# Mixer B's attention: far scores copied by ScalarE into p's row and masked there in one step, o summed in place, four row buffers

## Chip, cores and metric

The kernel runs on one core of a Trainium2 chip. The metric is device time in microseconds of one execution; the time before is the median of three runs.

## Reference

One decoder block over 1024 tokens of width 1024, float32. A combined projection feeds two attention mixers, their normed outputs go through one output projection, and a squared-ReLU MLP of width 4096 follows. The change touches the attention, above all mixer B: eight heads of 64, each query attending in three branches, at distances 0 to 128; at multiples of 4 up to 512; and at multiples of 16 up to 2048, mixed by their softmax denominators.

```python
B_BRANCHES = ((128, 1), (512, 4), (2048, 16))
...
for window, d in B_BRANCHES:
    sub = s // d
    ...
    o, lse = banded_attention(to_sub(q)[:, :, :, None, :], to_sub(k), to_sub(v),
                              window // d, return_lse=True)
...
w = jax.nn.softmax(jnp.stack(lses, axis=0), axis=0)
return jnp.sum(w[..., None] * jnp.stack(outs, axis=0), axis=0)
```

Mixing by denominators is one softmax over all keys in which a key counts as often as branches reach it (1, 2 or 3 times). The kernel does that with one additive mask: "neg" is 1e30 where no branch reaches, 0, −ln 2 or −ln 3 where one, two or three do. Scores are kept negated, so the row's maximum is a minimum, and the exponential uses scale −1.

## The kernel before

**Layout.** Tokens are stored in blocks of 128 with the even tokens of a block first and the odd ones behind. Far keys (two blocks back and more) are reached at even distances only, so of a far block a query in the even half needs the even 64 keys and one in the odd half the odd 64. The score matmul computes whole blocks into a PSUM bank (s_ps, up to 512 columns); from a far block only half is used. Near keys (this block and the one before, 256 columns) are used whole. A row of p for block qb therefore has 64 columns for each far block and 256 near ones, at most 640 in all.

**Work items.** Mixer A has 16 items (group, block); mixer B has 32 items (u, tp, h): a head pair u, a pair tp of query blocks (qb = 2 tp and 2 tp + 1), and a head h in the pair. For each of the two blocks qi of a mixer B item, `s_b` issues: the score matmuls (L1311) in one or two runs of up to four key blocks each, every run in its own bank of two; masking on VectorE (L1345); the exponential on ScalarE with the row's sum (L1353); the reciprocal on VectorE (L1356); and the scaling of p on GpSimd (L1358). `score_parts` splits the masking of a run: for far blocks one instruction for the 64 even rows and one for the 64 odd rows, since each half reads other columns of the bank; for the near blocks one instruction for all rows. Each adds the mask from SBUF to the scores in PSUM, writes p, and carries the running minimum on in "mn" (each leaves a short read-out of mn behind it). A query block with two runs so takes up to five such instructions.

Then `t_pv` follows in one or more chunks of up to 512 columns: TensorE transposes p (pt_ps, L1451), ScalarE rounds it to the high half of ph (L1462), VectorE subtracts to get the low half (L1466), and TensorE multiplies ph by the values (o_ps; L1481 near, L1490 far, L1500 for mixer A). The bank o_ps holds high and low parts in its two column halves (mixer B) and in its row halves. For mixer B, ScalarE copies rows 64 to 127 of the first 256 columns to otmp (L1525), VectorE adds the second 256 columns to it in place (L1529) and the first ones into ot (L1530), and a DMA stores ot to o_dram. Mixer A does it with one copy (L1541) and one add (L1546).

**Buffers.** p's rows: three (NP, r_p); score banks: two (r_s); ot: two (r_ot), and one otmp (r_tmp).

**What sets the order.** A planner inside the program (`Sched`) issues every instruction once, when the program is built. It keeps a clock for each engine, takes for each step a written-down cost (`t_dv(n)` for VectorE, `t_ps(n)` for ScalarE reading PSUM, and so on), and gives each engine next the step that could start first by these clocks. Each engine's queue then runs in the order so written. On TensorE the streams of scores, transposes and value products are mixed with "dense" steps (the input projection pj, later the output projection y_ps), which it prefers or puts back by how far attention has come. A step may name two engines and goes to the one that the planner finds done first; GpSimd has a bonus of 1.5 us there. So a changed cost, step or buffer count moves steps on all engines, also those that the change does not name: the subtractions w_hl of the input weights (L601) are such a step.

**The end.** `finish` (L2324) makes the last sums of each token block in two halves of 512 columns, and for each half sends two DMAs (L2333), one for the even and one for the odd tokens.

Of the kernel before, what the change touches and what calls it, by code (L numbers as in the profile page):

```python
# [19 lines left out]
P = 128  # L20
# [38 lines left out]
CW_MA = CW_MB + 1280  # L59
# [58 lines left out]
def _constants(c):  # L118
# [5 lines left out]
    for i in range(2):  # L124
        back = np.repeat(np.arange(6 + i, i, -1), 64)[None, :]
        far = P * back + 2 * (p % 64 - np.tile(np.arange(64), 6)[None, :])
        d = np.concatenate([np.where(back > 1, far, -1), near], 1)
        mult = ((d >= 0) & (d <= 128)).astype(int)
        mult += (d >= 0) & (d <= 512) & (d % 4 == 0)
        mult += (d >= 0) & (d % 16 == 0)  # L130
        c[:, CW_MB + 640 * i:CW_MB + 640 * i + 640] = neg[mult]
# [268 lines left out]
def hybrid_block(ctx: ExitStack, tc: tile.TileContext, x, positions, w_ada, b_ada, g_attn_post, w_in, w_out,  # L400
# [33 lines left out]
    WR, WS, NP, NV, NK, NQ, NT, NO = 6, 2, 3, 3, 2, 2, 2, 2  # L434
    NF = (1, 1)
    TILED = ()
# [5 lines left out]
    r_v, r_k, r_q, r_p, r_ph, r_ot, r_tmp = Res(NV), Res(0), Res(0), Res(NP), Res(NT), Res(NO), Res(1)  # L442
# [630 lines left out]
    def open_attention():  # L1073
# [14 lines left out]
        masks = mkp.tile([P, 1536], F32, name="masks")  # L1088
        e_mask = load(lambda: nc.sync.dma_start(masks[:], consts[:, CW_MB:CW_MB + 1536]), 786432, prio=-20)
        mask_b = [masks[:, 640 * i:640 * i + 640] for i in range(2)]  # L1090
        mask_a = masks[:, 1280:1536]
# [130 lines left out]
    def t_s(qb, run):  # L1222
        if qb // 2 in TILED:
            return (2 * t_mm(P * (qb // 2)) + 0.18) * (run == 0) + 2 * t_mm(2 * P) * (run == n_runs(qb) - 1)
        a, z = s_runs(qb)[run]
        return 2 * t_mm(P * (z - a))

    def n_runs(qb):
        if qb // 2 in TILED:
            return 2 if qb > 5 else 1  # L1230
        return len(s_runs(qb))
# [16 lines left out]
    UB = 2 * (sum(t_s(qb, r) for qb in range(TB) for r in range(n_runs(qb))) +  # L1248
# [21 lines left out]
    def s_b(i, it, rec):  # L1270
# [6 lines left out]
        for qi in range(2):  # L1277
# [4 lines left out]
            seen = [0, 0]  # L1282
            runs = n_runs(qb)
            for m in range(runs):
                end = m == runs - 1

                def f_s(m=m, qi=qi, qb=qb, w=w, b=b, end=end):
# [7 lines left out]
                    q = [qs[u, qb // 4][:, 2 * h + hl, qb % 4 * P:qb % 4 * P + P] for hl in range(2)]  # L1295
                    if tp in TILED:
                        keys = ks[u][:, h].rearrange("p (b c t) -> p b c t", c=2, t=64)
                        if m == 0:
                            for hl in range(2):
# [29 lines left out]
                for n_, (rows, to, from_, nb) in enumerate(parts):  # L1329
# [3 lines left out]
                    for c_ in range(2):  # L1333
                        seen[c_] += whole or c == c_
# [1067 lines left out]
```

## Time and profile before

| | us |
|---|---|
| median of 3 runs (lowest, highest) | 1112.0 (1110.38, 1113.53) |
| the profiled execution, its own time | 1110.98 |
| its span in the profile | 1109.2 |
| mean granted TensorE clock | 0.997 |

Line numbers L... are those of the program before unless the text says otherwise. In rows of the profile, PE is TensorE's matmuls, PEld its weight loads (which overlap them), DVE is VectorE, ACT ScalarE, POOL GpSimd, SP the queue that issues DMAs. A group's row has line, engine, operation, out<-in, shapes and count; then busy time in us and the mean of one in ns; then the idle time of the engine just before them, and what ended it. CUSTOM_DVE_ANT_0 at L1345 is the masking with its running minimum. A row of waits has who waited, for whom, us in all, how often, and the longest. A row of DMAs has what is moved, the count, the size of one and the median time from issue to landing in us. A row of the timeline has the start and the duration in us.

### The profile page before, as it was taken

Reading aid. Unit: us, or ns where it says so; the run is one execution under the profiler, and the core shown is the slowest. Engines: PE = TensorE matmul, PEld = TensorE weight load, DVE = VectorE, ACT = ScalarE, POOL = GpSimd, SP = SyncE. Lnnn points to the kernel's source line nnn. Section 1 sums busy time; section 2 is a strip of 40 time slices with the busy share of each in tenths; the row PEclk is TensorE's granted clock in tenths of the full one; section 3 lists DMA queues with packets and bytes.
Section 4 is the critical chain, followed back from the end, with each engine's and each line's share of the span. In section 5 each row is a group of like instructions: output and inputs, shape, how many; then the busy total and the mean of one; then the engine's idle time right before and its main releaser. Section 6 shows DMA issues by size and latency. Waiting matters only on the chain.

```text
span 1109.2 us, 15399 instructions
## 1 busy us (share of the span) xinstructions
PE 1086.1 (98%) x5185; PEld 894.8 (81%) x5185; DVE 840.3 (76%) x1616; ACT 614.2 (55%) x1080; POOL 246.8 (22%) x324
## 2 busy tenths in 40 slices
PE   8999999999999899999999999999999999999996
PEld 7788888888787777888888888888888888888885
DVE  7978688788888886689797664898644995537997
ACT  8768676464645556677675244743245632347442
POOL 2158777776642121210000000000000000000003
PEclk9999999999999999999999999999999999999998
DMA  9766677565634825657741379322578013593106
GB/s 350 214 197 196 194 213 238 188 205 165 209 115 147 273 84 171 216 221 263 276 164 38 126 254 346 137 77 76 202 269 296 1 57 119 195 330 135 38 20 152
DMA packets 97950, 198.65 MB, mean 179 GB/s; under 512 B 9776, under 2 KB 35504, under 8 KB 97872
## 3 DMA queue, kind: packets, MB, share of 16 engines
q1 hardware_dynamic: 97872, 197.68, 53.1%
q8 instruction: 41, 0.67, 0.3%
q14 instruction: 37, 0.30, 0.1%
HBM read 141.93 MB, written 33.03 MB: 158 GB/s over the span
## 4 chain that ended last, share of the span: by engine, by line
PE 71%; DVE 13%; DMA 6%; issue 4%; ACT 2%; POOL 2%; SPq 1%; POOLq 0%; DVEq 0%; ACTq 0%
PE mlp_ps L2212 17%; PE mlp_ps L2214 17%; PE mlp_ps L2213 17%; PE pj L978 3%; PE pj L981 3%; PE pj L979 3%; DVE p_sb L1345 2%; DMA wa<-in_w_ada 2%; PE s_ps L1311 2%; DMA o_sb<-o_dram 2%; DMA w_st<-in_w_in 1%; PE s_ps L1401 1%; PE y_ps L1766 1%; PE y_ps L1768 1%; PE y_ps L1767 1%
## 5 line engine op out<-in xcount | busy, mean ns | idle before, releaser
L2212 PE MATMUL mlp_ps<-hw 128*128 128x512 f32 x896 | 348.9, 389 | 0.1
L2213 PE MATMUL mlp_ps<-hw 128*128 128x512 f32 x896 | 348.6, 389 | 0.0
L2214 PE MATMUL mlp_ps<-hw 128*128 128x512 f32 x896 | 348.6, 389 | 0.0
L2214 PEld LDWEIGHTS mlp_ps<-hw 128*128 128x128 f32 x896 | 168.2, 188 | 35.2
L2213 PEld LDWEIGHTS mlp_ps<-hw 128*128 128x128 f32 x896 | 168.2, 188 | 35.1
L2212 PEld LDWEIGHTS mlp_ps<-hw 128*128 128x128 f32 x896 | 168.2, 188 | 35.1 <-DVE u L2249 0.6
L1976 DVE TENSOR_TENSOR hw<-w,hw 128x1024 fp32r<-128x1024 f32 x96 | 114.6, 1221 | 97.6 <-ACT hw L1969 95.9
L1969 ACT CAST hw<-w 128x1024 fp32r<-128x1024 f32 x96 | 97.7, 1048 | 127.5 <-PE mlp_ps L2214 86.8
L2322 POOL TENSOR_TENSOR st<-st,nhalf 128x1 f32<-128x1 f32 x8 | 8.0, 1010 | 591.8 <-DVE st L2320 591.8
L978 PE MATMUL pj<-hw,w_hl 128*128 128x512 f32 x240 | 99.3, 414 | 0.0
L981 PE MATMUL pj<-hw,w_hl 128*128 128x512 f32 x240 | 94.6, 394 | 0.0
L979 PE MATMUL pj<-hw,w_hl 128*128 128x512 f32 x240 | 94.3, 393 | 0.0
L1969 ACT CAST hw<-u 128x1024 fp32r<-128x1024 f32 x48 | 48.6, 1052 | 63.2 <-PE mlp_ps L2214 63.2
L1466 DVE TENSOR_TENSOR ph<-pt_ps,ph 128x512 fp32r<-128x512 f32 (+2 forms) x94 | 57.4, 628 | 22.2 <-ACT ph L1462 21.8
L1976 DVE TENSOR_TENSOR hw<-u,hw 128x1024 fp32r<-128x1024 f32 x48 | 56.9, 1219 | 17.8 <-ACT hw L1969 17.8
L1462 ACT CAST ph<-pt_ps 128x512 fp32r<-128x512 f32 (+2 forms) x94 | 49.1, 541 | 29.7 <-PE pt_ps L1451 25.7
L2270 DVE TENSOR_TENSOR yacc<-yacc,mlp_ps 128x512 f32<-128x512 f32 x96 | 62.0, 682 | 3.3 <-PE mlp_ps L2214 3.3
L1353 ACT ACTIVATE p_sb<-p_sb,mn 128x640 f32<-128x640 f32 (+3 forms) x64 | 42.0, 657 | 33.5 <-DVE mn L1345 30.8
L1358 POOL TENSOR_SCALAR p_sb<-p_sb,den 128x640 f32<-128x640 f32 (+3 forms) x64 | 39.8, 626 | 74.2 <-DVE den L1356 57.3
L1128 POOL TENSOR_TENSOR ada_acc<-ada_acc,wa_st 128x512 f32<-128x512 f32 x42 | 55.5, 1321 | 3.5
L981 PEld LDWEIGHTS pj<-hw,w_hl 128*128 128x128 f32 x240 | 45.1, 188 | 10.2
L1766 PE MATMUL y_ps<-hw,oh 128*128 128x512 f32 x128 | 52.1, 407 | 1.1 <-DVE mn L1345 0.7
(212 smaller groups left out, 1938.3 us busy)
## 6 DMA issues: line engine op xcount, KB each, us to landing
hw<-s_dram SPq DMA_DIRECT2D x84, 512.0 KB, 4.2
wa_st<-in_w_ada SPq DMA_DIRECT2D x32, 512.0 KB, 5.4
w<-in_w_up SPq DMA_DIRECT2D x32, 512.0 KB, 5.8
w<-in_w_down SPq DMA_DIRECT2D x32, 512.0 KB, 7.1
s_dram<-hw SPq DMA_DIRECT2D x28, 512.0 KB, 3.3
qt<-hl SPq DMA_DIRECT2D x40, 256.0 KB, 3.0
w_st<-in_w_in SPq DMA_DIRECT2D x36, 256.0 KB, 3.1
x_sb<-in_x SPq DMA_DIRECT2D x16, 512.0 KB, 5.6
```

The source lines that it names most:

```text
L978: T.matmul(ps, w[:, 0, n], h[0], start=(k == 0), stop=False)
L979: T.matmul(ps, w[:, 1, n], h[0], start=False, stop=False)
L981: T.matmul(ps, w[:, 0, n], h[1], start=False, stop=(k == KC - 1))
L1128: G.tensor_tensor(ada.acc[:, :512], ada.acc[:, :512], wa[:, j], ALU.add)
L1466: V.tensor_tensor(b["ph"][:, 1, :w], b["pt"][:, :w], b["ph"][:, 0, :w].bitcast(F32), ALU.subtract)
L1766: T.matmul(ps[:], b["oh"][:, k], wh[:, c0:c0 + 512], start=(k == 4 * m), stop=False)
L1969: A.copy(out[j][0], flat(src[j]))
L1976: V.tensor_tensor(out[j][1], flat(src[j]), out[j][0].bitcast(F32), ALU.subtract)
L2212: T.matmul(ps[m][:], sh, mh, start=starts and k == 0, stop=False, **kw)
L2213: T.matmul(ps[m][:], sh, ml_, start=False, stop=False, **kw)
L2214: T.matmul(ps[m][:], sl, mh, start=False, stop=k == 3, **kw)
L2270: e = op("DVE", t_dv(512), lambda: V.tensor_tensor(y(), y(), ps[m][:], ALU.add), [e, ml.e_y[tb, n]], gives=gives, prio=1)
```

## The change

- **Masking.** The far columns of each run are now copied by ScalarE, one instruction for the even rows and one for the odd rows, from the bank into p's row, unmasked and compact. The near columns are masked by VectorE from the bank for all rows, as before, but start the minimum anew. When all far copies and the near masking of the row are done, one VectorE instruction over all 128 rows adds the mask to the far columns in place and carries the minimum on. For that, both blocks of an item use one mask; the first block of an item has one far block less, and its unused 64 columns are filled with 1e30 by GpSimd. A bank that holds far blocks only is given back by the second copy; the last one by the near masking, which waits for the copies of its run.
- **o.** ScalarE copies rows 0 to 63 of all 512 columns into ot; VectorE adds rows 64 to 127 of the first 256 columns; then the second 256 columns of ot are added to the first, on VectorE or GpSimd as the planner finds. otmp is gone; mixer A uses ot in the same way.
- **Buffers.** Four for p's rows.
- **Masks.** One table of 640 columns less in the constants and in SBUF.
- **Output.** One DMA for each half of a token block.
- A switch that was off (TILED) is removed.

```diff
-CW_MA = CW_MB + 1280
+CW_MA = CW_MB + 640
...
-    WR, WS, NP, NV, NK, NQ, NT, NO = 6, 2, 3, 3, 2, 2, 2, 2
+    WR, WS, NP, NV, NK, NQ, NT, NO = 6, 2, 4, 3, 2, 2, 2, 2
...
-        masks = mkp.tile([P, 1536], F32, name="masks")
+        masks = mkp.tile([P, 896], F32, name="masks")
...
-                        V.tensor_tensor_reduce(p, src, msk, 1.0, mn[:, n0 - 1:n0] if n0 else BIG, ALU.add, ALU.min,
-                                               mn[:, n0:n0 + 1])
-                    last = n_ == len(parts) - 1
-                    last_mn = op("DVE", t_dv(nb) + 0.06, f_max, [e, e_mask] + ([last_mn] if last_mn else []),
-                                 gives=[(r_s, 1)] if last else [], prio=1)
...
+                far = min(z, qb - 1) - a if tp else 0
+                if far > 0:
+                    for c in range(2):
+                        def f_far(c=c, a=a, far=far, m=m, qi=qi, b=b):
+                            rows = slice(64 * c, 64 * c + 64)
+                            A.copy(rec.p[qi][rows, 64 * a:64 * (a + far)].rearrange("p (b t) -> p b t", t=64),
+                                   b["s", m][rows].rearrange("p (b c t) -> p b c t", c=2, t=64)[:, 0:far, c])
+                        e = op("ACT", t_ps(64 * far) + 0.13, f_far, [e], gives=[(r_s, 1)] if c and not end else [], prio=1)
+                    e_far.append(e)
+                if end:
...
+                        V.tensor_tensor_reduce(rec.p[qi][:, o:w], b["s", m][:, c0:c0 + n], mask_b[:, 640 - w + o:640],
+                                               1.0, BIG, ALU.add, ALU.min, b["mn"][:, 0:1])
+                    last_mn = op("DVE", t_dv(w - o) + 0.2, f_near, [e, e_mask], gives=[(r_s, 1)], prio=1)
+            if tp:
+                n = 64 * (qb - 1)
+                if not qi:
+                    e_far.append(op("POOL", 0.2, lambda n=n: G.memset(rec.p[0][:, n:n + 64], BIG), [e], prio=1))
+
+                def f_max(qi=qi, w=w, b=b, n=n):
+                    V.tensor_tensor_reduce(rec.p[qi][:, 0:n], rec.p[qi][:, 0:n], mask_b[:, 384 - n:384],
+                                           1.0, b["mn"][:, 0:1], ALU.add, ALU.min, b["mn"][:, 1:2])
+                last_mn = op("DVE", t_dv(n) + 0.16, f_max, [last_mn] + e_far, prio=1)
...
-                A.copy(ob["tmp"][:, :256], rec.o[64:128, :256])
+                ob["ot"] = opool.tile([64, 512], F32, name="ot", tag="ot")
+                A.copy(ob["ot"][:], rec.o[0:64])
...
-                V.tensor_tensor(ob["tmp"][:, :256], rec.o[0:64, 256:512], ob["tmp"][:, :256], ALU.add)
-                V.tensor_tensor(ob["ot"][:], rec.o[0:64, :256], ob["tmp"][:, :256], ALU.add)
...
+                V.tensor_tensor(ob["ot"][:, :256], rec.o[64:128, :256], ob["ot"][:, :256], ALU.add)
+
+            def f_o3(eng):
+                return lambda: eng.tensor_tensor(ob["ot"][:, :256], ob["ot"][:, :256], ob["ot"][:, 256:], ALU.add)
...
+            e = op(("DVE", "POOL"), (t_dv(256) + 0.08, t_ptt(256)), (f_o3(V), f_o3(G)), [e], prio=0)
...
-                for c in range(2):
-                    nc.sync.dma_start(dst[c], s.x[64 * c:64 * c + 64, 512 * hf:512 * hf + 512])
+                nc.sync.dma_start(dst, s.x[:, 512 * hf:512 * hf + 512])
```

**VectorE, early in mixer B**, in the program before: the first block (qb = 4) of the item u = 2, tp = 2, h = 0, with its two runs. ISA rows with p_sb are maskings, ISA rows with mn alone their read-outs.

```order
L1345 ISA p_sb,mn<-s_ps,masks 64x192
L1345 ISA mn 64x1
L1345 ISA p_sb,mn<-s_ps,masks 64x192
L1345 ISA mn 64x1
L1345 ISA p_sb,mn<-s_ps,masks,mn 64x64
L1345 ISA mn 64x1
L1345 ISA p_sb,mn<-s_ps,masks,mn 64x64
L1345 ISA mn 64x1
L1529 TENSOR_TENSOR otmp<-o_ps,otmp 64x256
L1530 TENSOR_TENSOR ot<-o_ps,otmp 64x256
L1345 ISA p_sb,mn<-s_ps,masks,mn 128x256
L1345 ISA mn 128x1
```

The same block in the changed program (its own line numbers: L1321 is the near masking, L1330 the one over the far columns, L1492 the add to ot, L598 a subtraction of w_hl):

```order
L1321 ISA p_sb,mn<-s_ps,masks 128x256
L1321 ISA mn 128x1
L598 TENSOR_TENSOR w_hl<-w_st,w_hl 128x512
L1492 TENSOR_TENSOR ot<-o_ps,ot 64x256
L1556 SCALAR_TENSOR_TENSOR wo_st<-wo_st,head,wo_hi 128x1024
L1330 ISA p_sb,mn<-p_sb,masks,mn 128x192
L1330 ISA mn 128x1
```

Five maskings became two, the second with both operands in SBUF, and the second add of o is no longer here.

**ScalarE at the same place**, before: the cast of v_hl of the same projection step, then casts of p (ph), a copy of o (otmp) and exponentials.

```order
L946 CAST v_hl<-pv 128x8x64
L1462 CAST ph<-pt_ps 128x512
L1525 COPY otmp<-o_ps 64x256
L596 CAST w_hl<-w_st 128x512
L1353 ACTIVATE p_sb,den<-p_sb,mn 128x512
```

In the changed program (L1311 there is the copy of far scores, L1489 the copy of o, L1336 the exponential):

```order
L943 CAST v_hl<-pv 128x8x64
L1426 CAST ph<-pt_ps 128x512
L593 CAST w_hl<-w_st 128x512
L1311 COPY p_sb<-s_ps 64x192 x2
L1489 COPY ot<-o_ps 64x512
L1552 ACTIVATE wo_hi<-wo_st,head 128x1024
L1311 COPY p_sb<-s_ps 64x256 x2
L1336 ACTIVATE p_sb,den<-p_sb,mn 128x512
```

Pairs of far copies stand between the casts and the exponentials, and the copy of o has 512 columns.

More of the change, by code (lines that the diff above doesn't have):

```diff
@@ L1539, in f_o1 @@
             def f_o1():
[L1540 to L1542 removed]
+                ob["ot"] = opool.tile([64, 512], F32, name="ot", tag="ot")
+                A.copy(ob["ot"][:], rec.o[64:128])
             def f_o2():
[L1545 to L1547 removed]
+                V.tensor_tensor(ob["ot"][:], rec.o[0:64], ob["ot"][:], ALU.add)
+            e0 = op("ACT", t_ps(512), f_o1, [ep], takes=[(r_ot, 1)], prio=0)
+            e = op("DVE", t_dv(512), f_o2, [e0], gives=[(r_ob, 1)], prio=0)
             def f_st():
```

112 lines of the change are left out of this document (27 added, 85 removed).

## The prediction

> **What bounds the kernel now.** I read the page first, then the busy time by stage, then what TensorE waited for, and only then the durations of the pieces that the change touches.
>
> ```profile
> span 1109.2 us, 15399 instructions
> PE 1086.1 (98%) x5185; PEld 894.8 (81%) x5185; DVE 840.3 (76%) x1616; ACT 614.2 (55%) x1080; POOL 246.8 (22%) x324
> 60.00:166.00 106.00, 105.50 (x578) 87.95 (x576) 81.38 (x223) 77.48 (x216) 79.01 (x121) 1.00 0.68 203
> 166.00:430.00 264.00, 257.58 (x1361) 210.79 (x1359) 215.14 (x718) 148.31 (x316) 132.11 (x153) 1.00 0.55 177
> 430.00:512.00 82.00, 80.37 (x385) 65.78 (x383) 60.58 (x99) 59.30 (x99) 10.96 (x14) 1.00 0.57 205
> 512.00:1100.00 588.00, 586.99 (x2588) 485.47 (x2587) 430.81 (x470) 280.08 (x383) 9.23 (x9) 1.00 0.47 163
> 560.00:600.00 40.00, 40.00 (x178) 33.10 (x178) 35.66 (x35) 23.85 (x32) 0.00 (x0) 1.00 0.26 88
> ```
>
> The columns of the window rows are PE, PEld, DVE, ACT and POOL busy, then clock and DMA. TensorE is busy throughout; mixer A's attention fills about 60 to 166, mixer B's 166 to 430, the output projection 430 to 512, the MLP the rest. The change removes no matmul, so it can only win TensorE's idle time before 512 and the tail after the last matmul. In mixer B's stage that idle time is 264.00 − 257.58 = 6.4 us. It understates the waits: 178 matmuls of 512 columns go in 40 us, one per 0.225 us, yet the record of each lasts 0.389 us (below), so a start may be 0.164 us late before idle time shows.
>
> ```profile
> L2212 PE MATMUL mlp_ps<-hw 128*128 128x512 f32 x896 | 348.9, 389 | 0.1
> 166.27 0.41 PE L1311 MATMUL s_ps<-kt,qt 128*128 128x128 f32 x2
> 166.97 0.50 PE L1500 MATMUL o_ps<-ph,v_hl 128*128 128x512 f32 x1 [0.30 <-DVE v_hl L949]
> ...
> 398.41 0.39 PE L1768 MATMUL y_ps<-hw,ol 128*128 128x512 f32 x1
> 398.86 0.50 PE L1311 MATMUL s_ps<-kt,qt 128*128 128x512 f32 x1
> ```
>
> From the first to the last of these places, 26 starts come over 0.14 us late by the timeline; 6.4 + 26 × 0.164 = **10.7 us** is what TensorE loses in mixer B's stage, and the most that the attention edits can win there. The weight loads name the causes:
>
> ```profile
> PEld o_ps L1481 <- DVE ph L1466: 3.9, 6, 1.3
> PEld s_ps L1311 <- issue: 3.3, 9, 0.6
> PEld s_ps L1311 <- DVE mn L1345: 2.5, 6, 0.8
> PEld o_ps L1490 <- DVE ph L1466: 1.4, 3, 1.0
> PEld pt_ps L1451 <- POOL p_sb L1358: 1.3, 5, 0.3
> ```
>
> Two are VectorE's: 2.5 us for a score bank that the masking (mn L1345) has not yet emptied, and 3.9 + 1.4 = 5.3 us for ph, the low half of p, which stands in VectorE's queue behind such masking. Waiting for p itself costs only 1.3.
>
> **The change part by part: VectorE.** Its rows in mixer B:
>
> ```profile
> L1345 DVE CUSTOM_DVE_ANT_0 p_sb<-s_ps,masks,mn 128x256 f32<-128x256 f32 x48 | 22.8, 477 | 1.8 <-PE s_ps L1311 0.7
> L1345 DVE CUSTOM_DVE_ANT_0 p_sb<-s_ps,masks 64x256 f32<-64x256 f32 x48 | 20.2, 420 | 2.5 <-PE s_ps L1311 1.6
> L1345 DVE CUSTOM_DVE_ANT_0 p_sb<-s_ps,masks,mn 64x128 f32<-64x128 f32 x32 | 11.1, 347 | 1.4 <-PE s_ps L1311 0.7
> L1345 DVE CUSTOM_DVE_ANT_0 p_sb<-s_ps,masks 64x128 f32<-64x128 f32 x32 | 9.0, 286 | 1.1 <-PE s_ps L1311 0.6
> L1345 DVE CUSTOM_DVE_ANT_0 p_sb<-s_ps,masks 64x192 f32<-64x192 f32 x16 | 5.6, 353 | 0.5 <-PE s_ps L1311 0.3
> L1345 DVE CUSTOM_DVE_ANT_0 p_sb<-s_ps,masks,mn 64x64 f32<-64x64 f32 x16 | 4.5, 282 | 0.5
> L1345 DVE CUSTOM_DVE_ANT_0 p_sb<-s_ps,masks 128x256 f32<-128x256 f32 x8 | 3.3, 413 | 0.0
> L1345 DVE CUSTOM_DVE_ANT_0 p_sb<-s_ps,masks 128x128 f32<-128x128 f32 x8 | 2.2, 278 | 0.0
> L1530 DVE TENSOR_TENSOR ot<-o_ps,otmp 64x256 f32<-64x256 f32 x32 | 13.3, 417 | 1.1
> ```
>
> - The 144 half-row maskings go: 20.2 + 11.1 + 9.0 + 5.6 + 4.5 = 50.4 us. The 48 near ones lose their carried minimum: 48 × (477 − 413) ns = 3.1 us.
> - 48 whole-row maskings from SBUF come, eight each of 64, 128, ... 384 columns. No row shows one that reads two SBUF operands; the 128-row forms above give 143 ns + 1.055 ns a column (413 and 278) plus 64 ns for the carried minimum: 8 × (6 × 207 + 1.055 × 1344) ns = 21.3 us.
> - Of the 32 second adds of o, 27 stand in GpSimd's program now: −27 × 417 ns = −11.3 us. Five more w_hl subtractions stand in VectorE's instead, 0.69 us each when undisturbed (18.75 below): +3.4 us.
>
> Net −50.4 − 3.1 + 21.3 − 11.3 + 3.4 = −40.1 us: from 215.1 to 175 of 264 us, 81% to 66%.
>
> **ScalarE** gains 128 copies of half rows, and its copy of o grows from 256 to 512 columns:
>
> ```profile
> L1525 ACT COPY otmp<-o_ps 64x256 f32<-64x256 f32 x32 | 11.8, 369 | 17.4 <-PE o_ps L1490 13.4 <-PE o_ps L1481 3.3 <-DVE ot L1530 0.3
> L1541 ACT COPY otmp<-o_ps 64x512 f32<-64x512 f32 x16 | 9.3, 583 | 8.3 <-PE o_ps L1500 8.1
> ```
>
> That is 155 ns + 0.836 ns a column: 48 × 369 + 16 × 315 + 32 × 262 + 32 × 209 ns = 37.8 us, and 32 × 214 ns = 6.8 us. The copies gather every second 64 columns; the maskings of the same views cost no more than contiguous ones (420 against 413 ns), so I add nothing. ScalarE goes from 148.3 to 193 us, 73%: still beside TensorE.
>
> **GpSimd** gains 27 adds of 64 x 256 and 24 fills of 64 columns. Nearest rows: an add of 128 x 512 at 1332 ns, which bounds one from above; I take half, 0.67, and 0.2 for a fill: 23 us, so 132.1 becomes some 150 with the five subtractions gone (5 × 1.3). It is off the path unless it holds others up, and there the trace has something to say:
>
> ```profile
> 18.75 0.69 DVE L601 TENSOR_TENSOR w_hl<-w_st,w_hl 128x512 fp32r<-128x512 f32 x1
> 230.34 1.79 DVE L601 TENSOR_TENSOR w_hl<-w_st,w_hl 128x512 fp32r<-128x512 f32 x1
> 229.93 1.65 POOL L1128 TENSOR_TENSOR ada_acc<-ada_acc,wa_st 128x512 f32<-128x512 f32 x1
> L1128 POOL TENSOR_TENSOR ada_acc<-ada_acc,wa_st 128x512 f32<-128x512 f32 x28 | 37.3, 1332 | 2.3
> ```
>
> The same subtraction of two SBUF tiles takes 0.69 us with GpSimd idle, and 1.79 when a GpSimd add is running: it ends 0.55 us after that add (231.58 to 232.13). The old maskings read one operand from PSUM; the new whole-row ones read p and the mask, both in SBUF. Each may so wait for what GpSimd is doing: GpSimd is busy half the stage (132.11 of 264), its mean piece is 132.11 / 153 = 0.86 us, so 0.5 × 0.43 = 0.21 us on average and 1.33 at worst; 48 × 0.21 = 10 us. VectorE then stands at 185 of 264, 70%, still under today's 81%.
>
> [...]
>
> **What of this lies on the path.** Score-bank waits, 2.5 us: a bank is now emptied by two ScalarE copies (2 × 369 ns where there were 2 × 420), the last one by two copies and one near masking (2 × 262 + 413 where there were 2 × 347 + 477). Bounds: all of it gone, or as much again if the copies queue behind exponentials; I take −2.5, since VectorE no longer holds the first bank at all. Waits for ph, 5.3 us: they pass ScalarE (its cast) and then VectorE (its subtraction); one gets fuller, the other emptier. Bounds: all gone, −5.3; or later, for in the changed program 17 of the 48 whole-row maskings stand at most two rows ahead of such a subtraction, 17 × 0.21 = +3.6 us by the mean hold-up (17 × 1.33 = 22.6 if every one met the longest piece). I take −0.9, nearer to nothing. The fourth row buffer lets scores run further ahead; p is waited for only 1.3 us, and I count nothing. The loads of the masks (768 to 448 KB) delay no row of TensorE: nothing.
>
> **Tail.** The last output piece is ready at 1104.41; its two DMAs start at 1105.07 and, half of 1.19 later, at 1105.66, behind two others in SP's queue:
>
> ```profile
> 1103.67 0.74 DVE L2324 SCALAR_TENSOR_TENSOR x_sb<-yg,st,x_sb 128x512 f32<-128x512 f32 x1
> 1105.07 1.19 SPq L2333 DMA_DIRECT2D out_x<-x_sb  x2
> out_x<-x_sb SPq DMA_DIRECT2D x32, 128.0 KB, 2.3
> gate_d<-gate_st SPq DMA_DIRECT2D x4, 256.0 KB, 2.8
> ```
>
> One DMA of 256 KB can go at about 1104.5, 1.15 us before the last one of today (1105.66), and lands in 2.8 instead of 2.3: −0.6 us (0 to −1.2).
>
> **Sum.** The profiled execution took 1110.98 us, 1.8 more than its span and 1.0 under the median of the three runs (1112.0; they span 1110.38 to 1113.53), so I leave it uncorrected. 1110.98 − 2.5 − 0.9 − 0.6 = **1107.0 us**. A measurement of this kernel can tell about 0.3%, 3.3 us, from no change; the forecast lies just beyond.
>
> **The rivals.**
> - *The waits only change their names.* ScalarE at 73% takes VectorE's place ahead of ph and of the banks. For it: the waits on "issue" (3.3) and on p stay, and what VectorE loses ScalarE gains nearly one for one (40 and 45 us). Against: no engine would be as full as VectorE is today. Only the tail is won: 1110.4.
> - *Slower: the whole-row masking waits for GpSimd.* Its place is the first part of mixer B, where GpSimd runs 0.76 and 1.3 us pieces of the modulation; its price 17 × 0.21 = 3.6 us of late ph, and nothing won but the tail: 1110.98 + 3.6 − 0.6 = 1114.0. It decides from the point where a held masking plus the subtraction behind it outlasts the matmuls scheduled before o_ps, as the present waits of up to 1.3 us show to be close. Against: VectorE gets 40 us shorter. [...]
> - *All of it goes.* Both VectorE waits and those they carry along vanish, 10.7 us, with the tail: 1099.7. Against: 3.3 us of it is put down to issue.
>
> **How the numbers follow.** Forecast 0.45, unchanged 0.30, slower 0.15, all gone 0.10. Around the forecast its own bounds spread several us, so some four fifths of its chance lies beyond 0.3%: faster 0.37 + 0.10 = 0.47; same 0.08 + 0.28 + 0.02 = 0.38, and slower 0.13 + 0.02 = 0.15, since the slower case may stay within 0.3% (0.02) and the unchanged one may end late (0.02). The range, 1101.0 to 1114.5, leaves out the last rival and the far end of the slower one.
>
> **What the profile will show.** The forecast is right if VectorE in mixer B's stage is near 185 us, ScalarE near 193, the wait of s_ps for mn gone, and the last output DMA starts within 0.2 us of its data. Whole-row maskings much over 0.21 us longer than 143 + 64 + 1.055 a column, ending with GpSimd's pieces, show the hold-up; TensorE's waits for ph above 5.3 us make the prediction wrong on the slow side, new waits for the score copies leave it at no change.

## The result: 5% slower, and all of it behind the last matmul

| | before | changed |
|---|---|---|
| median of 4 runs, us | 1111.19 (1109.29 to 1113.53) | 1167.36 (1167.09 to 1167.69) |
| ratio to before, 95% interval | 1 | 1.0505 (1.0483 to 1.0526) |
| profiled execution, us | 1110.98 | 1167.15 |
| its span, us | 1109.2 | 1165.4 |
| mean granted TensorE clock | 0.997 | 0.972 |

The prediction was 1107.0 us, with a range up to 1114.5: wrong by 60 us and in sign. Line numbers from here on are those of the changed program, unless a row is said to be of another.

The page of the changed kernel, its first lines and the DMA share in 40 slices of the span:

```profile
span 1165.4 us, 15326 instructions
PE 1083.3 (93%) x5185; PEld 894.3 (77%) x5185; DVE 819.0 (70%) x1406; ACT 652.7 (56%) x1208; POOL 266.4 (23%) x366
DMA  9665777463638345667315781336931258410111
```

TensorE is busy for as long as before (1083.3 against 1086.1 us); the span grew around it. The DMA row tells where: the last three slices, some 87 us, all stand at a tenth, right where the output is stored. The stages next (window, its length, then PE, PEld, DVE, ACT, POOL busy, granted clock, DMA share, GB/s):

```profile
60.00:166.00 106.00, 105.45 (x580) 87.98 (x579) 81.49 (x231) 80.60 (x223) 78.11 (x119) 1.00 0.68 208
166.00:430.00 264.00, 256.81 (x1370) 212.31 (x1369) 194.27 (x501) 187.33 (x445) 153.53 (x197) 1.00 0.54 176
430.00:512.00 82.00, 81.62 (x386) 66.79 (x385) 62.77 (x102) 58.75 (x93) 10.05 (x15) 1.00 0.59 214
1100.00:1165.00 65.00, 0.00 (x0) 0.00 (x0) 1.41 (x2) 0.00 (x0) 0.08 (x1) 0.50 0.13 50
```

Up to 512 us TensorE's busy time differs little from before. In the last 65 us the engines do nothing but the last sums, and the DMA engines run at 13% and 50 GB/s. The granted clock of 0.50 there belongs to an idle TensorE, and that is what pulls the mean down to 0.972; where TensorE works it is 1.00, so the clock is no cause. The end in the timeline, the changed kernel's last matmul, its last sum and then SP's queue in which the output DMAs are issued; below them the last matmul of before:

```profile
1095.86 0.39 PE L2179 MATMUL mlp_ps<-hw 128*128 128x512 f32 x1
1100.78 0.74 DVE L2289 SCALAR_TENSOR_TENSOR x_sb<-yg,st,x_sb 128x512 f32<-128x512 f32 x1
L2297 SPq DMA_DIRECT2D out_x<-x_sb x16: 534/4949/7156, 1079.3 to 1145.8; - x16
```

```profile
1098.73 0.39 PE L2214 MATMUL mlp_ps<-hw 128*128 128x512 f32 x1
L2333 SPq DMA_DIRECT2D out_x<-x_sb x32: 466/571/597, 1082.2 to 1105.7; - x32
```

(The rows on out_x give an instruction's shortest, median and longest duration in ns, and its first and last start.) The last matmul ends at 1096.25, 2.9 us *earlier* than before (1099.12), and the last sum is ready at 1101.52. (That alone is no gain: in three other executions of the same attention program, below, the last matmul ends anywhere from 1093.9 to 1099.8.) But an output DMA that held SP's queue for 571 ns now holds it for 4949, and the last of the 16 is issued at 1145.8, 44 us behind its data. Their bytes account for the end: 16 × 256 KB are 4.19 MB, and at the 51 GB/s of the window 1105 to 1145 that is 82 us; counted from the first issue, 1079.3 + 82 = 1161, and the span ends at 1165.4.

```profile
1105.00:1145.00 40.00, 0.00 (x0) 0.00 (x0) 0.00 (x0) 0.00 (x0) 0.00 (x0) 0.50 0.13 51
```

A share of 0.13 is that of 2 of the 16 engines (0.125). The output view is `out[...].rearrange("(t c) d -> c t d", c=2)`: its outermost dimension counts the two halves, c = 2. The suspicion: a DMA whose outermost dimension has two entries runs on two engines.

### The profile page after: what moved, and what is told of

It reads as the page before. It is cut to its first block, busy times and chain, and to the rows that moved or that the text cites. A ratio compares the mean times of both kernels' runs of the same rounds, so it can differ in the third digit from the quotient of the medians.

```text
span 1165.4 us, 15326 instructions
## 1 busy us (share of the span) xinstructions
PE 1083.3 (93%) x5185; PEld 894.3 (77%) x5185; DVE 819.0 (70%) x1406; ACT 652.7 (56%) x1208; POOL 266.4 (23%) x366
## 4 chain that ended last, share of the span: by engine, by line
PE 75%; DVE 9%; DMA 4%; issue 3%; ACT 2%; POOL 1%; SPq 0%; POOLq 0%; DVEq 0%; ACTq 0%
PE mlp_ps L2177 16%; PE mlp_ps L2179 16%; PE mlp_ps L2178 16%; PE pj L975 4%; PE pj L978 4%; PE pj L976 4%; PE s_ps L1287 2%; PE y_ps L1731 2%; PE y_ps L1733 2%; PE y_ps L1732 2%; DMA wa<-in_w_ada 1%; PE s_ps L1365 1%; PE pt_ps L1415 1%; PE o_ps L1464 1%; PE pt_ps L1419 1%
## 5 line engine op out<-in xcount | busy, mean ns | idle before, releaser
L1430 DVE TENSOR_TENSOR ph<-pt_ps,ph 128x512 fp32r<-128x512 f32 (+2 forms) x94 | 58.3, 630 | 20.9 <-ACT ph L1426 20.2
L1341 POOL TENSOR_SCALAR p_sb<-p_sb,den 128x640 f32<-128x640 f32 (+3 forms) x64 | 44.6, 701 | 40.2 <-DVE den L1339 32.1
L1733 PE MATMUL y_ps<-hw,ol 128*128 128x512 f32 x128 | 50.2, 392 | 0.5 <-DVE ol L1690 0.5
```

Of the source, the lines that this page charges most:

```text
L1430: V.tensor_tensor(b["ph"][:, 1, :w], b["pt"][:, :w], b["ph"][:, 0, :w].bitcast(F32), ALU.subtract)
L1733: T.matmul(ps[:], b["ol"][:, k], wh[:, c0:c0 + 512], start=False, stop=(k == 4 * m + 3))
```

## The experiments

**First question: is it the one output DMA, and nothing else?** Two kernels split the change: e1_two has all of it but that DMA, e2_one has that DMA alone.

e1_two, against the changed kernel:

```diff
-                nc.sync.dma_start(dst, s.x[:, 512 * hf:512 * hf + 512])
+                for c in range(2):
+                    nc.sync.dma_start(dst[c], s.x[64 * c:64 * c + 64, 512 * hf:512 * hf + 512])
```

> The changed kernel with the output sent as before (two DMAs of 64 rows for each half). Theory A (the single output DMA, whose slowest dimension has 2 entries, runs on 2 of the 16 DMA engines and makes the whole loss; the attention edits gain): last matmul near 1096 us as in the changed kernel, output done some 9 us after it, 1108 us, 0.997 of before. Theory B (the changed order leaves the end of the MLP with late sums or loads, and the queue only shows it): stays near 1167.

Measured: 1108.5 us median (1105.77 to 1111.32), 0.9990 of before (0.9978 to 1.0002). The 59 us are gone. Whether the rest of the change gains anything isn't clear of the noise: 0.997 was expected, and the interval reaches past 1.

e2_one, against the kernel before:

```diff
-                for c in range(2):
-                    nc.sync.dma_start(dst[c], s.x[64 * c:64 * c + 64, 512 * hf:512 * hf + 512])
+                nc.sync.dma_start(dst, s.x[:, 512 * hf:512 * hf + 512])
```

> The kernel before with only the output DMAs made single. Theory A: all of the loss and none of the gain, about 5 us in SP's queue for each of the last DMAs, near 1169 us. Theory B: within 2 us of before, near 1111.

Measured: 1169.4 us (1168.21 to 1170.58), 1.0529 of before (1.0512 to 1.0546). The same 12 us of the end, first in e2_one, then in the kernel before:

```profile
1096.00:1108.00 12.00, 3.72 (x17) 2.75 (x15) 8.56 (x16) 2.17 (x6) 2.85 (x3) 0.77 0.13 51
```

```profile
1096.00:1108.00 12.00, 3.12 (x14) 2.25 (x12) 7.97 (x16) 1.64 (x6) 2.85 (x3) 0.74 0.76 175
```

One line changed, and 76% and 175 GB/s became 13% and 51. The DMA costs the 5% alone, whatever the attention does.

**Is it the size of a DMA or its leading dimension?** e3_rows keeps 256 KB in one DMA, but of 64 whole rows, so that the leading dimension is 64; it sends both when the second half of the token block is ready.

```diff
-                dst = out[tb * P:(tb + 1) * P, 512 * hf:512 * hf + 512].rearrange("(t c) d -> c t d", c=2)
-                nc.sync.dma_start(dst, s.x[:, 512 * hf:512 * hf + 512])
+                dst = out[tb * P:(tb + 1) * P].rearrange("(t c) d -> c t d", c=2)
+                for c in range(2):
+                    nc.sync.dma_start(dst[c], s.x[64 * c:64 * c + 64])
```

> The changed kernel with half as many output DMAs in another way: two for each token block, of 64 rows and 4 KB a row, when both halves are ready. Theory A: 64 entries lead, so all 16 engines take part; each DMA 256 KB as in the changed kernel, yet issued in about 0.6 us; 1107 to 1108.5 us. A rival (256 KB in one output DMA is too much for a queue): about 5 us in the queue for each again, over 1150.

Measured: 1108.85 us (1107.63 to 1112.14), 0.9986 of before (0.9975 to 0.9996). As many bytes in a DMA as in the changed kernel, as many DMAs, and none of the loss: it is the leading dimension and not the size. (The rows of these DMAs are 4 KB and not 2 KB; but those of e1_two are 2 KB, with a leading 64, and it has none of the loss either.)

**How does the rate go with it?** e4_dose is the kernel before with its store and reload of x2 (512 KB for each of the eight token blocks, a scratch tensor of its own) written with leading dimensions of 128, 2, 4, 8, 16, 32, 64 and 128.

```diff
+    LEAD2 = [128, 2, 4, 8, 16, 32, 64, 128]
...
-        e_x2[tb] = load(lambda: nc.sync.dma_start(x2_dram[tb][:], b["y"][:]), 524288, [e], prio=-2)
+        e_x2[tb] = load(lambda: nc.sync.dma_start(x2_at(tb), b["y"][:]), 524288, [e], prio=-2)
...
-                nc.sync.dma_start(s.x[:], x2_dram[tb][:])
+                nc.sync.dma_start(s.x[:], x2_at(tb))
```

> The kernel before with x2's scratch in DRAM laid out so that the slowest dimension of its store and its load has 128, 2, 4, 8, 16, 32, 64, 128 entries for token blocks 0 to 7 (the same 512 KB and the same 4 KB rows each). Theory A: the time in the DMA engines goes as 1 over min(entries, 16): about 20 us with 2 entries, 10 with 4, 5 with 8, and the 3 to 4 us of today from 16 on; the landing writes 2, 4, 8, 16 completion packets. Rival (rows and strides, not engines): all alike, 3.1 us.

Measured, one run: 1132.9 us. Four windows: the store with 2 entries alone, the store with 4 alone, and twice the reloads, when a few engines are left with the rest of them.

```profile
419.00:426.00 7.00, 3.76 (x21) 2.89 (x19) 1.31 (x3) 0.00 (x0) 0.00 (x0) 1.00 0.13 53
445.00:447.00 2.00, 2.00 (x15) 1.74 (x14) 1.07 (x3) 0.18 (x1) 0.00 (x0) 1.00 0.24 74
1043.00:1047.00 4.00, 4.00 (x19) 3.33 (x18) 1.66 (x2) 3.97 (x8) 0.00 (x0) 1.00 0.12 34
1048.00:1049.50 1.50, 1.50 (x8) 1.25 (x7) 1.50 (x2) 1.09 (x2) 0.00 (x0) 1.00 0.13 52
```

In the two stores 0.13 is two sixteenths and 0.24 is four: with 2 and with 4 the leading dimension is the number of engines. Which of the reloads are under way in the last two windows can't be read from them. The times expected were partly a miss: the packets of the 2-entry store ran for 11.6 us (415.1 to 426.7) and not 20 (512 KB at 53 GB/s are 10 us), four engines moved 74 GB/s and not twice 53, and the larger doses lie beside other transfers and can't be read by themselves. The count of packets fits the expected landing: 9708 under 512 B where before has 9776, and 2, 4 and 8 in place of 16 for the store and the reload give 2 × (14 + 12 + 8) = 68 fewer. (e3_rows, with a leading 64, has 256 fewer for its 16 fewer DMAs, 16 each.) So the number of busy engines is shown for 2 and 4, and a time of 1 over that number is not.

**Second question: why did the attention bring so little?** Without the output DMA the change is at 0.9990, some 1.1 us, where the prediction counted 3.4. The whole-row masking can be held up by GpSimd; e5_nolock, against e1_two, takes its second SBUF operand away (it adds no mask to the far scores and does not carry the near minimum on, so it leaves out a part of the attention):

```diff
-                    V.tensor_tensor_reduce(rec.p[qi][:, 0:n], rec.p[qi][:, 0:n], mask_b[:, 384 - n:384],
-                                           1.0, b["mn"][:, 0:1], ALU.add, ALU.min, b["mn"][:, 1:2])
+                    V.tensor_reduce(b["mn"][:, 1:2], rec.p[qi][:, 0:n], axis=mybir.AxisListType.X, op=ALU.min)
```

> The changed kernel with two output DMAs, and in the whole-row step over the far columns only a minimum over p (one SBUF operand; the mask is not added there and the near minimum is not carried on, so far weights are left unmasked). The order of all instructions is that of the two-DMA kernel. Theory L (the hold-up by GpSimd, 10 us of VectorE time in the changed kernel, is what eats the attention gain): waits of TensorE over 0.14 us in mixer B fall from about 11 to 7 us, and the time to some 0.996 of before, 1105.5. Theory N (ScalarE and VectorE only trade places ahead of ph; the hold-up is covered): same time as with two DMAs, 0.999 of before, and waits for ph as large as there.

Measured: 1104.85 us (1103.68 to 1106.56), 0.9952 of before (0.9939 to 0.9966), so some 4 us under e1_two. The groups of this step in mixer B's stage, four sizes in the changed kernel and two of them in e5_nolock:

```profile
L1330 DVE CUSTOM_DVE_ANT_0 p_sb<-p_sb,masks,mn 128x320 f32<-128x320 f32 x8 | 6.7, 836 | 0.2
L1330 DVE CUSTOM_DVE_ANT_0 p_sb<-p_sb,masks,mn 128x256 f32<-128x256 f32 x8 | 5.7, 715 | 1.4 <-ACT p_sb L1311 1.2
L1330 DVE CUSTOM_DVE_ANT_0 p_sb<-p_sb,masks,mn 128x128 f32<-128x128 f32 x8 | 4.9, 618 | 0.1
L1330 DVE CUSTOM_DVE_ANT_0 p_sb<-p_sb,masks,mn 128x64 f32<-128x64 f32 x8 | 3.9, 487 | 0.2
```

```profile
L1330 DVE TENSOR_REDUCE mn<-p_sb 128x1 f32<-128x320 f32 x8 | 3.8, 478 | 0.0
L1330 DVE TENSOR_REDUCE mn<-p_sb 128x1 f32<-128x64 f32 x8 | 1.7, 211 | 0.0
```

The masking's means lie far above the line (618 ns for 128 columns, where 64 + 143 + 1.055 × 128 = 342 was worked out; 715 for 256, where it is 477): that is waiting inside the instruction. The fastest of each size are within 10 ns of the line, 22 of the 48 are 0.07 to 1.03 us above it, and at the start of each of the 22 a GpSimd instruction is running. The masking then ends behind that instruction by its own worked-out length less some 0.2 us (0.18 to 0.21), in all 22: in these a start of 0.2 us ran beside GpSimd, and the rest waited for its end. Of 13 more that start under GpSimd and are not held, 12 find at most 0.19 us of its instruction left; at 262.30 the GpSimd add had begun 0.09 us before, and it was the add that took long (1.84 us, median 1.29). None of the 13 that start with GpSimd idle is longer than the line by more than 0.05 us. Its busy time over all 48 is 31.2 us in the changed kernel, 9.9 over the 21.3 worked out for undisturbed ones. One such wait from its cause to TensorE, in the changed kernel's timeline:

```profile
259.62 1.60 POOL L1125 TENSOR_TENSOR ada_acc<-ada_acc,wa_st 128x512 f32<-128x512 f32 x1
260.00 1.57 DVE L1330 CUSTOM_DVE_ANT_0 p_sb<-p_sb,masks,mn 128x320 f32<-128x320 f32 x1
261.50 0.42 DVE L1321 CUSTOM_DVE_ANT_0 p_sb<-s_ps,masks 128x256 f32<-128x256 f32 x1
261.98 0.19 PEld L1287 LDWEIGHTS s_ps<-kt,qt 128*128 128x128 f32 x1 [0.85 <-DVE mn L1321]
```

A GpSimd add ends at 261.22; the masking that came 0.38 us behind it ends at 261.57, though 320 columns want 0.54. VectorE's next instruction empties a score bank, late; and TensorE's weight load waits 0.85 us for that bank. The wait that the change was to remove (for mn) is back, at the near masking, because of what stands ahead of it. (Not all of the lateness is the masking's: the subtraction ahead of it, L870, had taken 2.13 us.) The e5_nolock gain of 4 us is not the hold-up alone: its minimum takes 18.1 us for all 48, so of the 12.8 us less than in e1_two (31.0) some 9.7 were hold-up and 3.1 the carried minimum's own time.

**Which part of the change does what?** e6_np3 is e1_two with three row buffers in place of four; e7_mask is the kernel before with the copies and the whole-row masking alone; e8_osum is the kernel before with the new sum of o alone.

```diff
-    WR, WS, NP, NV, NK, NQ, NT, NO = 6, 2, 4, 3, 2, 2, 2, 2
+    WR, WS, NP, NV, NK, NQ, NT, NO = 6, 2, 3, 3, 2, 2, 2, 2
```

> The changed kernel with two output DMAs and three row buffers instead of four. If the fourth buffer carries the gain in mixer A and the output projection (some 2 us less waiting in the profiles), 1110 or more; if it does nothing, as with four, 0.999 of before.

Measured: 1109.63 us, 1.0000 of before (0.9991 to 1.0009). The fourth buffer is worth about 0.1%, and the intervals of this and of e1_two overlap.

e7_mask, against before (the new masking as in the diff of the change; otmp, the sum of o, three row buffers and two output DMAs as before):

```diff
+                            A.copy(rec.p[qi][rows, 64 * a:64 * (a + far)].rearrange("p (b t) -> p b t", t=64),
+                                   b["s", m][rows].rearrange("p (b c t) -> p b c t", c=2, t=64)[:, 0:far, c])
...
+                    V.tensor_tensor_reduce(rec.p[qi][:, 0:n], rec.p[qi][:, 0:n], mask_b[:, 384 - n:384],
+                                           1.0, b["mn"][:, 0:1], ALU.add, ALU.min, b["mn"][:, 1:2])
```

> The kernel before with the far copies and the whole-row masking alone (old sum of o, three buffers, two output DMAs). Theory L: the hold-up costs more than the 29 us that VectorE is spared are worth, 1.000 to 1.003 of before. Theory N: within 0.1% of before either way. If the masking were the gain: 0.997 or less.

Measured: 1114.43 us, 1.0043 of before (1.0030 to 1.0055): slower, alone, and by more than the 1.003 that the dearest of its expectations allowed.

e8_osum, against before (the masking as before):

```diff
-                A.copy(ob["tmp"][:, :256], rec.o[64:128, :256])
+                A.copy(ob["ot"][:], rec.o[0:64])
...
+                V.tensor_tensor(ob["ot"][:, :256], rec.o[64:128, :256], ob["ot"][:, :256], ALU.add)
...
+            e = op(("DVE", "POOL"), (t_dv(256) + 0.08, t_ptt(256)), (f_o3(V), f_o3(G)), [e], prio=0)
```

> The kernel before with the sum of o in place and partly on GpSimd alone. Both theories: within 0.2% of before; the bank of o is given back one add earlier, which TensorE waits for nowhere.

Measured: 1119.79 us, 1.0090 of before (1.0076 to 1.0104). A clear miss: 0.2% either way was expected. The weight loads' waits from 160 to 520 us, in e8_osum (its line numbers are near those of before):

```profile
PEld s_ps L1311 <- issue: 7.7, 12, 1.6
PEld o_ps L1481 <- DVE ph L1466: 4.6, 7, 1.2
PEld o_ps L1490 <- DMA v_far<-v_hl: 2.7, 2, 1.7
PEld o_ps L1490 <- DVE ph L1466: 2.6, 6, 0.7
```

No single wait is the loss: "issue" at the scores went from 3.3 to 7.7, ph from 5.3 to 7.2, and a wait for a DMA of values is new. To tell GpSimd's part from the rest, two more kernels put all 32 last sums of o on VectorE: e12_osumv is e8_osum so changed, e13_twov is e1_two.

```diff
-            e = op(("DVE", "POOL"), (t_dv(256) + 0.08, t_ptt(256)), (f_o3(V), f_o3(G)), [e], prio=0)
+            e = op("DVE", t_dv(256) + 0.08, f_o3(V), [e], prio=0)
```

> The program of e8_osum (before with the in-place o sum alone), but the last sum of o, which reads and writes ot alone, stands always on VectorE: none of the 32 on GpSimd. e8_osum is at 1.009 of before. If GpSimd's part costs it (25 adds of 762 ns in one queue with the scalings of p and the modulation, each delaying those behind it, and a changed order of what else GpSimd gets), this goes back to near 1.000 (0.997 to 1.003). If the new order that the planner makes for the in-place form costs it, on whichever engine the last sum is, it stays at 1.006 or above. VectorE then has 25 adds more, which GpSimd can hold up (845 ns each in e8_osum): if that is what matters it gets slower than e8_osum.

> The program of e1_two (the whole change with two output DMAs), but all 32 last sums of o on VectorE. If GpSimd's taking 27 of them is what the change gains by, this is slower than e1_two (0.999) by the 27 x 0.5 us of VectorE's time that comes back, of which a part reaches TensorE: 1.000 to 1.004. If VectorE has room enough, since the masking left it, no change from e1_two: 0.998 to 1.000.

Measured: e12_osumv 1119.3 us, 1.0078 of before (1.0063 to 1.0093), so nearly all of e8_osum's loss is there without GpSimd. e13_twov 1110.12 us, 1.0006 (0.9995 to 1.0018), just inside the first of its two expectations; the interval reaches into the second, so GpSimd's share is worth some 0.16% to the whole change, if anything. The five last sums that VectorE kept in the changed kernel took 1050 ns each, those of e13_twov 519. These few too were waiting for GpSimd: each of the four long ones (974 to 1497 ns) starts under a GpSimd add and ends some 0.28 us after it, and most of e13_twov's take 396 to 424 ns.

```profile
L1495 DVE TENSOR_TENSOR ot<-ot 64x256 f32<-64x256 f32 x5 | 5.3, 1050 | 0.1
```

```profile
L1495 DVE TENSOR_TENSOR ot<-ot 64x256 f32<-64x256 f32 x32 | 16.6, 519 | 0.4
```

What TensorE loses by stage, from the timeline of each profiled execution: the sum of the starts that come over 0.14 us later than the usual spacing after a matmul of that width (0.2265 us for 512 columns), in us.

| kernel | mixer A | mixer B | output projection | whole time against before |
|---|---|---|---|---|
| before | 1.4 | 10.7 | 2.1 | 1 |
| e11_btail (same attention) | 1.4 | 10.1 | 2.5 | 0.9993 |
| changed | 0.6 | 11.0 | 0.7 | 1.0505 |
| e1_two (same attention) | 0.6 | 9.2 | 0.7 | 0.9990 |
| e3_rows (same attention) | 0.7 | 12.9 | 0.7 | 0.9986 |
| e10_tail (same attention) | 0.6 | 10.8 | 1.6 | 0.9979 |
| e5_nolock | 0.6 | 8.5 | 0.7 | 0.9952 |
| e6_np3 | 1.4 | 11.9 | 1.3 | 1.0000 |
| e13_twov | 0.6 | 12.0 | 2.3 | 1.0006 |
| e7_mask | 1.5 | 16.0 | 1.1 | 1.0043 |
| e8_osum | 1.4 | 20.9 | 0.9 | 1.0090 |
| e12_osumv | 1.4 | 19.9 | 0.7 | 1.0078 |

The four kernels with the change's attention spread from 9.2 to 12.9 us in mixer B, around the 10.7 of before: mixer B itself won nothing that can be seen. What is smaller in all four is the output projection, 0.7 to 1.6 us against 2.1 and 2.5 in the two with the attention of before. The 0.8 us in mixer A are no gain. A stage ends here where the next one's first scores start, and with four row buffers mixer B's first scores (L1287) come before two matmuls of the modulation (ada_ps) that cost 0.6 us by this measure, so that these count in mixer B; before, they stand in mixer A, whose stage ends at 166.27. The changed kernel, then before:

```profile
161.28 0.62 PE L1287 MATMUL s_ps<-kt,qt 128*128 128x128 f32 x4
161.74 1.02 PE L1143 MATMUL ada_ps<-ada_acc,ones 128*128 128x512 f32 x2
```

```profile
154.12 1.02 PE L1146 MATMUL ada_ps<-ada_acc,ones 128*128 128x512 f32 x2
```

**A part of the losses came at half the clock.** In mixer B's window (166 to 430) the mean granted clock was 1.00 before, but 0.98 in e7_mask, 0.99 in e8_osum and e3_rows and 0.97 in e12_osumv. Their traces have stretches of 3.4 or 6.8 us there at a clock of 0.50, in which most matmuls of 512 columns start 0.43 us apart and not 0.2265: 10.2 us of them in e7_mask, 13.7 in e12_osumv, 3.4 in e8_osum and in e3_rows. Half the clock can cost at most half of that, 5.1, 6.8 and 1.7 us (an estimate from these lengths), and in e7_mask that could be the whole loss of 4.7 us. Each stretch begins during a late start of TensorE of 1 to 4 us or within 2 us of its end, though not every such wait is followed by one; why the clock falls isn't shown. The longest wait, e7_mask's, is a matmul of the output projection that waits for VectorE's sums over o_sb, and not for a masking; the window behind it is at half the clock:

```profile
388.22 0.98 PE L1702 MATMUL pm_o<-ones,o_sb 128*128 128x1 f32 x4 [3.80 <-DVE o_sb L1696]
389.00:393.00 4.00, 4.00 (x10) 3.18 (x11) 0.86 (x4) 0.92 (x2) 1.82 (x2) 0.50 0.34 103
```

All five runs of e7_mask have a mean clock of 0.991 to 0.995 and all four of e12_osumv one of 0.992 to 0.994, where the runs of before have 0.995 to 0.998.

**Third question: what can the tail give?** e10_tail is e1_two, and e11_btail the kernel before, with the odd rows of the last token block issued from ScalarE's queue:

```diff
-                    nc.sync.dma_start(dst[c], s.x[64 * c:64 * c + 64, 512 * hf:512 * hf + 512])
+                    eng = nc.scalar if c and tb == TB - 1 else nc.sync
+                    eng.dma_start(dst[c], s.x[64 * c:64 * c + 64, 512 * hf:512 * hf + 512])
```

> The program of e1_two again, but of the last token block's output the DMAs of the odd rows are issued from ScalarE's queue, beside SP's. In e1_two and before, the two DMAs of the last piece start about 0.6 us apart in SP's queue and the first waits for two others. If the end is set by SP's issuing (0.5 to 0.6 us each), the last output issue comes some 1.2 us sooner and the time is 0.6 to 1.2 us under e1_two: near 0.998 of the kernel before. Rival: the end is set by the landing of the last 128 KB whichever queue issues it, or ScalarE's queue takes over the delay: no change from e1_two, 0.999. A gain under 1 us shows in the trace only, as a shorter stretch from the last matmul to the end of the span.

> The kernel before, with nothing changed but the same: the last token block's DMAs of the odd rows are issued from ScalarE's queue. It measures the tail by itself, which the prediction took at 0 to -1.2 us for one DMA in place of two. By SP's issuing as the cause: the last output issue stands right behind its data, 0.6 to 1.2 us less than before (0.9990 to 0.9995). Rival: no change, 1.000.

Measured: e10_tail 1107.9 us, 0.9979 of before (0.9967 to 0.9990); e11_btail 1109.62 us, 0.9993 (0.9983 to 1.0002). In e11_btail's timeline the last sum and the two issues from ScalarE's queue:

```profile
1103.13 0.75 DVE L2324 SCALAR_TENSOR_TENSOR x_sb<-yg,st,x_sb 128x512 f32<-128x512 f32 x1
1103.25 1.46 ACTq L2334 DMA_DIRECT2D out_x<-x_sb  x2
```

Two issues of some 0.6 us end at 1104.71, 0.83 behind the last sum (1103.88); before, the last ended 1.85 behind it (1104.41 to 1106.26). From the last matmul's end to the end of the span it is 9.13 us (1098.60 to 1107.73), where it was 10.04 (1099.12 to 1109.17). The other traces agree: this stretch is 10.0 us in all eight kernels that send 128 KB at a time from SP's queue alone, and 9.1 and 9.2 in the two that use ScalarE's as well. The second reading, that the landing alone sets the end, falls in the traces; e11_btail's interval by itself would still allow it. e10_tail has the lowest median of the kernels that compute the whole block; its interval lies under 1, but overlaps that of e1_two.

## Why the prediction was wrong

**The step that failed is the tail.** It read: "One DMA of 256 KB can go at about 1104.5, 1.15 us before the last one of today (1105.66), and lands in 2.8 instead of 2.3: −0.6 us (0 to −1.2)." The 2.8 us came from the row of gate_d<-gate_st, 256 KB as well; but that DMA's tensors lead with 128 partitions, and the output view leads with c = 2. Bytes were taken for the price, and the access pattern set it: +59 us (1167.36 − 1108.5), shown by leaving it out (e1_two), by making it alone (e2_one), and by the same bytes with a leading 64 (e3_rows). No bound and no rival of the prediction held it: every case kept the DMA's cost within a microsecond. "Slower" had a chance of 0.15, for another reason (the hold-up by GpSimd); that the time came out slower owes nothing to that rival.

In the runs a leading 2 gave 0.13 of the engines, 4 gave 0.24, and 64 lost nothing (0.9986 of before). No row of before shows that count. With the two engines that the runs show, rows of before give an estimate of the end: two of the sixteen, at the 175 GB/s and 0.76 share of the last 12 us, carry 175 × 0.125 / 0.76 = 29 GB/s, by which 4.19 MB take 144 us behind 1079, where the span had 30 left. At the 51 GB/s that two engines then moved it was 82 us.

**The tail's size was right for another mechanism.** An issue right behind its data was to win 0 to 1.2 us; with two queues (e11_btail) it won 0.9 in the trace, and 0.0007 of the time, which is not clear of the noise. For one DMA of 256 KB, as the prediction had it, nothing bears it out.

**The instruction costs were right, the sum for VectorE was not.** ScalarE was to be at 193 us in mixer B's stage and is at 187.33, GpSimd at 150 and is at 153.53. VectorE was to be near 185 with the hold-up and is at 194.27 (192.74 in e1_two), 20.9 under before and not 30. The busy times of its groups of instructions in that window add up to 246.6 us before and 213.8 after, 32.8 less, but the busy column counts a stretch in which two instructions overlap once: 215.14 and 194.27. The prediction took a sum of durations off a busy time. (The 32.8 also hold 7.5 us for 98 read-outs of mn that it hadn't listed. Without them it is 25.3, where 30 was forecast; the largest part of that gap is the five last sums of o, 5.3 us where 417 ns each make 2.1.) The hold-up itself was put at 10 us on 48 instructions and measured 9.9: 22 of them were held, by 0.45 us on average, where half of them and 0.43 had been taken. That both fit is in part luck, for GpSimd was running at the start of 35, and 12 of these had at most 0.19 us of it left. Where the prediction said "may", the trace shows it: 22 of the 48 maskings with both inputs in SBUF waited for the end of a GpSimd instruction, all but their first 0.2 us, as the plain subtraction at 230.34 had (1.79 us where 0.69 is usual). The near maskings, which read PSUM, took at most 426 ns (median 416), though GpSimd was busy for 153.53 of the 264 us.

**The path was half wrong.** Of the terms for TensorE's waits, −2.5 at the banks and −0.9 at ph, these came:

```profile
PEld o_ps L1445 <- DVE ph L1430: 5.5, 9, 1.3
PEld o_ps L1454 <- DVE ph L1430: 2.6, 8, 0.6
PEld s_ps L1287 <- DVE mn L1321: 1.7, 3, 0.8
PEld s_ps L1287 <- ACT p_sb L1311: 0.9, 1, 0.9
```

The banks' wait for VectorE fell by 0.8 and not by 2.5, and 0.9 of waiting for ScalarE's copies came in its place: −2.5 was taken as if the near masking that empties the last bank could not be held, but it stands in one queue with the whole-row steps that are. ph went from 5.3 up to 8.1: +2.8 where −0.9 was taken, near the bound of +3.6 that the mean hold-up gave. In the three other executions of the same program ph is 7.0, 9.8 and 7.7 (e1_two, e3_rows, e10_tail), and the banks' wait for VectorE 0.8, 1.7 and 1.7. The text's own sign for "wrong on the slow side" (ph above 5.3) is there in all four. With e5_nolock ph is 5.4 and the time some 4 us less: what the prediction called the slower rival was the mechanism at work in mixer B, at about the size it gave, and it ate what the 20.9 us less of busy VectorE had brought. It did not make the attention slower than before. What met it is at least in part the wait of the scores on "issue", 3.3 us before, which the prediction took to stay: none of the four executions has a row of it. Why it went isn't shown.

```profile
PEld o_ps L1444 <- DVE ph L1429: 3.5, 8, 1.2
PEld o_ps L1453 <- DVE ph L1429: 1.9, 6, 0.6
```

(The two rows are e5_nolock's, whose lines stand one higher.) The fourth row buffer, for which the prediction counted nothing, shows nothing clear of the noise: 0.9990 with four and 1.0000 with three, and in mixer A 0.2 us once the two matmuls of ada_ps are counted alike.

**What stays open.** The parts alone cost 0.4% (masking) and 0.8 to 0.9% (the sum of o), yet together nothing, with four row buffers (e1_two) as with three (e6_np3). GpSimd isn't the reason for the second (e12_osumv). Each edit lets the planner write another order, the half clock can add to such losses (at most 5.1 us in e7_mask by the estimate above), and in e8_osum several waits grew together; which of them leads, or whether ot being held from the copy on is the cause, was not tried. Nor was the masking's loss alone split into the hold-up, the new order and the clock.

## What to carry to other kernels

Before two DMAs are merged into one, read the outermost dimension of the merged view in DRAM. Here a transfer with a leading 2 had 0.13 of the 16 engines and 51 to 53 GB/s as a store, one with a leading 4 had 0.24 and 74 GB/s, and 256 KB with a leading 64 cost nothing; the row of another DMA of equal bytes, 2.8 us, was no price for the one with the leading 2. When work is moved off a PSUM operand so that both inputs of a VectorE instruction lie in SBUF, price the time that GpSimd may hold it (here 22 of 48 by 0.45 us on average), and add that to everything queued behind it. In a kernel whose order a planner writes, test an edit in the whole and alone: two edits that cost 0.4% and 0.9% alone cost nothing together (0.9990 and 1.0000 of before).

## What the hardware showed besides

- **The slow DMA showed in the issuing queue too.** SP's queue was held for a median of 4.9 us at each issue (0.57 before), about the 5.1 us in which two engines at 51 GB/s move the 256 KB of one such DMA. Here only the end of the program stood behind them.
- **Landing times were missing where such DMAs ran.** The profiles of the changed kernel and of e2_one give none for any DMA. Of e4_dose's eight stores of x2 only two have one, the fifth and the sixth with 16 and 32 entries (4.5 and 3.4 us), so their median of 3.9 says nothing about the 2-entry one, whose packets run for 11.6 us. The DMA share of a window (0.13) shows what the landing time does not.
- **A reload with 16 entries landed late behind slow ones.** In e4_dose the reload of the fifth block (16 entries), issued at 1029.67 right after those with 2, 4 and 8, landed 22.5 us later by the profile; the two others that have a landing time, with 64 and 128 entries, took 3.9 and 3.2. What held it wasn't tried.
- **At the share of two engines (0.12 to 0.13) the DMAs carried 51 to 53 GB/s as a store, and 34 and then 52 GB/s in two windows of the reloads**, so the number of engines is not all. The direction isn't the reason, with 52 beside 34; what slowed the first of the two windows wasn't tried.
- **The same attention program loses from 9.2 to 12.9 us in mixer B** in the profiled executions of four kernels that issue its instructions in the same order, as much spread as the gains that were forecast, and up to 1.7 us of the 12.9 came at half the clock. Only repeated timing decided at this size.
